# Squares on GpSimd, spread forms and a later S5 tile at the start of a hybrid decoder layer

## The chip, the cores and the metric

The kernel runs on one core of a Trainium2 chip. Its metric is the device time of one execution in microseconds (us), as the median of several executions. Five engines work side by side, each through its own instructions in order: TensorE (PE: matmuls, with PEld for its weight loads), VectorE (DVE), ScalarE (ACT), GpSimd (POOL) and SyncE (SP, which only issues transfers). ScalarE and GpSimd issue transfers as well.

## The reference

One layer of a decoder on 1024 prompt tokens and 8 sample tokens (1032 columns here), all in float32:

```python
h = rmsnorm(x, g_pre)                       # x * rsqrt(mean(x^2) + 1e-6) * g_pre, D = 2048
proj = h @ w_in                             # 2048 x 10240
q, k, v, za, ub, zb, ga, gb = split(proj)   # 4 x 1024, 2 x 1024, 2 x 2048 columns
ya = (retention(q, k, v) * silu(za)) @ w_pa
yb = (s5(ub) * silu(zb)) @ w_pb
out = (sigmoid(ga) * ya + sigmoid(gb) * yb) @ w_out
y = x + rmsnorm(out, g_post)
```

The states of retention and S5 are outputs too.

## The kernel before, in words

Activations lie transposed: a row tile is 128 features by 1032 tokens, and k counts the 16 such tiles of D. Each float32 product is made of three matmuls on rounded halves: a value is split into `hi` (a ScalarE copy that rounds) and `lo` (VectorE, value minus `hi`), and `three` issues hi x hi, hi x lo and lo x hi. Weights come as quarters of 128 x 512 (four k) and are split in the same way by `wtile`, into three rotating buffers a, b, c. The copy of a quarter can run once the matmuls of the quarter three before it are done.

Most of the kernel (`product`, line 984) multiplies with a Strassen-like scheme of seven products, which needs seven *forms* of the operands (`FORMS`: u1, t2, v1, t3, t1, t4, v2): halves of row tiles and sums and differences of them. What the change touches lies ahead of it, in the first 175 us:

1. The start stage (lines 382 to 411). It loads the 16 row tiles of x in the order `FX_ORDER`, splits each with the gain `g_pre` (L396 on ScalarE, L397 on VectorE), squares it on ScalarE (`sq`, L402, two buffers) and adds the square to `ssq`. TensorE multiplies each k at once with the weights of ub tiles 0 and 1 (weight tile j = 0, then j = 1, nine matmuls each). The normalisation is applied afterwards, as a scaling of the results by `rstd`. Six buffers `fx` hold row tiles; the last six stay for the forms.
2. `first_rms`, a generator of background work, computes `rstd`: nine small matmuls that read `ssq` (L461), a power on GpSimd (L467), two diagonal tiles on VectorE, matmuls that broadcast them (L477, L483), copies into `rstd`.
3. The second pair of row tiles: `linear` for ub tiles 2 and 3, four weight quarters each. After every third of the columns, and again at the end of a quarter, `slot()` runs the next piece of background work, up to its next `yield`: four slots a quarter, 32 in all. First `first_rms` runs in these slots and then `build_forms(0, ...)`. For each of four pairs of row tiles (u, v) that scales them (L423), makes t1 to t4 in four buffers `fo` (`tt`, counted as line 85), and stores seven forms to `fm_d`: u1, v1 and v2 by GpSimd's queue (L433), the t forms by ScalarE's (L437). Two row tiles, k = 0 and 3, are loaded again (`reload_a`, L448). After the first and the second pair, `scale_ub` scales ub tile 0 and ub tile 1 and stores it to `ub_d` for the S5 branch (L368); ub tiles 2 and 3 are stored by L351.
4. The v loop (`ps2`, lines 1309 to 1324): two tiles of v in eight quarters, with a slot at the end of each. Its background work is `first_forms`: it loads forms of the first half of K into ten buffers `stg` (`stage`, L923), waits four slots, and then splits four forms in a slot (`unstage`, L274), into the places that the row tiles of x leave. Product n of the first step (seven products) reads the n-th group of four.
5. The first step of `product`, from 157 us on; `first_forms` ends in its slots.

`slot()` lets background work be placed on TensorE, VectorE, ScalarE and SyncE only after the last foreground instruction there:

```python
def slot():
    with ExitStack() as after:
        for ins in anchor.values():
            after.enter_context(tc.issue_after(ins))
        while bg:
            try:
                next(bg[0])
                return
            except StopIteration:
                bg.popleft()
```

There is no such order for GpSimd. A helper such as `add` has all its instructions under line 85.

Of the kernel before, what the change touches and what calls it, by code (L numbers as in the profile page):

```python
# [10 lines left out]
F32 = mybir.dt.float32  # L11
F32R = mybir.dt.float32r
I32 = mybir.dt.int32
AF = mybir.ActivationFunctionType
ALU = mybir.AluOpType
# [3 lines left out]
D = 2048  # L19
SEQ = 1024  # L20
NB = 8
TOK = SEQ + NB
KD = D // 128
H = 8
G = 64
EPS = 1e-6
# [53 lines left out]
def emit(ctx, tc, I, O):  # L80
    nc = tc.nc
    V, A, P, T = nc.vector, nc.scalar, nc.gpsimd, nc.tensor
# [7 lines left out]
    def add(out, a, b, eng=None):  # L90
        return tt(out, a, b, ALU.add, eng)
# [16 lines left out]
    def st_tile():  # L108
        return stage_of["pool"].tile([128, stage_of["w"]], F32, name="st")
# [34 lines left out]
    fm_d = dram("fm_d", [2, 7, 4, 128, HT])  # L144
# [27 lines left out]
# [10 lines that stand above are left out]
# [54 lines left out]
    def misc():  # L236
        return banks_of["pms"].tile([128, 512], F32, name="misc")
# [90 lines left out]
    ubp = {}  # L328
# [5 lines left out]
        return t.rearrange("p (c s) -> p c s", s=8)  # L334

    def ub_new(j):
        u = ubp[j] = ubw.tile([128, 8, 144], F32, name="ubp")
        P.memset(u[:, 1:8, 0:8], 0.0)
        P.memset(u[:, 0:7, 136:144], 0.0)
        return u  # L340
# [22 lines left out]
    def scale_ub(j):  # L363
        u = ubp[j]
        mul(perm(u, 0, 128), perm(u, 0, 128), cs(rstd[:, 0:SEQ]))
        mul(u[:, 0, 0:8], u[:, 0, 0:8], rstd[:, SEQ:TOK])
        mul(u[:, 7, 136:144], u[:, 7, 136:144], rstd[:, SEQ:TOK])
        P.dma_start(ub_d[j * 128:(j + 1) * 128], u)  # L368
# [3 lines left out]

    s5stack = ExitStack()
    ubstack = ExitStack()
    ubw = ubstack.enter_context(tc.tile_pool(name="ubw", bufs=3))
    rm = ubstack.enter_context(tc.tile_pool(name="rm", bufs=1))
    ssq = rm.tile([128, TOK], F32, name="ssq")
    fx = ubstack.enter_context(tc.tile_pool(name="fxa", bufs=6))
    FX_ORDER = list(range(8, KD)) + [0, 3, 1, 2, 4, 5, 6, 7]
    kept = {}  # L380

    with tc.tile_pool(name="start", bufs=3) as sp:
        banks = [[mmbank() for _ in range(3)], [mmbank(), mmbank(), misc()]]
        w = None
        sqs = deque()
        for z, k in enumerate(FX_ORDER):
            xr = kept[k] = fx.tile([128, TOK], F32, name="fx")
            xh, xl = x_of(k)
            parts = THIRDS[0:3] if z == 0 else [(0, TOK)]
            for n, (a, b) in enumerate(parts):  # L390
                nc.sync.dma_start(xr[:, a:b], I["xT"][k, :, a:b])
                if z % 4 == 0 and n == 0:
                    w = [wquarter(w_in, M_UB, k // 4)]
                if z % 4 == 0 and n == len(parts) - 1:
                    w.append(wquarter(w_in, M_UB + 1, k // 4))
                A.activation(xh[:, a:b], xr[:, a:b], AF.Copy, scale=gpre[:, k:k + 1])  # L396
                V.scalar_tensor_tensor(xl[:, a:b], xr[:, a:b], gpre[:, k:k + 1], xh[:, a:b].bitcast(F32), ALU.mult, ALU.subtract)  # L397
            if z == 0:
                A.activation(ssq, xr, AF.Square)
            else:  # L400
                sqs.append(sp.tile([128, TOK], F32, name="sq", bufs=2))
                A.activation(sqs[-1], xr, AF.Square)  # L402
            for j in range(2):
                for t, (t0, t1) in enumerate(THIRDS[0:3]):
                    three(banks[j][t][:, 0:t1 - t0], w[j], k % 4, x_of(k), t0, t1, z == 0, z == KD - 1)
            if z > 1:
                add(ssq, ssq, sqs.popleft())
        add(ssq, ssq, sqs.popleft())
        for j in range(2):
            for t, (t0, t1) in enumerate(THIRDS[0:3]):  # L410
                evac_ub_raw(j, t, banks[j][t][:, 0:t1 - t0])
# [3 lines left out]
    def build_forms(kh, order, load, pool, fos, eng, after=()):  # L415
        raw = dict(kept) if not kh else {}
        load(raw, 0)
        yield
        for z, j in enumerate(order):
            t = {}  # L420
            for n, k in (("u", 8 * kh + j), ("v", 8 * kh + 4 + j)):
                r = raw.pop(k)
                V.scalar_tensor_tensor(r, r, gpre[:, k:k + 1], rstd, ALU.mult, ALU.mult)  # L423
                t[n + "1"], t[n + "2"] = r[:, 0:HT], r[:, HT:TOK]
            yield
            for n, a, b, op in (("t1", "u1", "u2", ALU.subtract), ("t3", "u2", "v2", ALU.subtract),
                                ("t2", "v2", "t1", ALU.add), ("t4", "v1", "t2", ALU.subtract)):
                t[n] = pool.tile([128, HT], F32, name="fo", bufs=fos)
                tt(t[n], t[a], t[b], op)
                if n == "t3":  # L430
                    for p, f in enumerate(FORMS):
                        if f in ("u1", "v1", "v2"):
                            eng.dma_start(fm_d[kh, p, j], t[f])  # L433
                    yield
            for p, n in enumerate(FORMS):
                if n[0] == "t":
                    A.dma_start(fm_d[kh, p, j], t[n])  # L437
            yield
            load(raw, z + 1)
            if z < len(after):  # L440
                after[z]()
            yield
# [10 lines left out]
                raw[k] = fb2.tile([128, TOK], F32, name="fx", bufs=4)  # L453
                P.dma_start(raw[k], I["xT"][k])

    def first_rms():
        n_ch = [(c, min(c + 128, TOK)) for c in range(0, TOK, 128)]
        r = TOK % 128
        ps = misc()
        for i, (a, b) in enumerate(n_ch):  # L460
            T.matmul(ps[0:b - a, i:i + 1], ssq[:, a:b], onesk, start=True, stop=True)  # L461
        ms, rs, hf = (rm.tile([128, 9], F32, name=n) for n in ("ms", "rs", "hf"))
        V.memset(ms, 1.0)
        V.memset(hf, -0.5)
        V.tensor_scalar(ms[:, 0:8], ps[:, 0:8], EPS, None, ALU.add)
        V.tensor_scalar(ms[0:r, 8:9], ps[0:r, 8:9], EPS, None, ALU.add)
        P.tensor_tensor(rs, ms, hf, ALU.pow)  # L467
        yield
        dg = [st_tile()[:, 0:512] for _ in range(2)]
        for i, d in enumerate(dg):  # L470
            V.scalar_tensor_tensor(d.rearrange("p (j c) -> p j c", c=128), ident.unsqueeze(1).broadcast_to([128, 4, 128]), float(D),
                                   rs[:, 4 * i:4 * i + 4].unsqueeze(2).broadcast_to([128, 4, 128]), ALU.mult, ALU.mult)
        yield
        yield
        for i, d in enumerate(dg):
            pb = misc()
            T.matmul(pb, onesk.broadcast_to([128, 128]), d, start=True, stop=True)  # L477
            V.tensor_copy(rstd[:, 512 * i:512 * i + 512], pb)
        d = st_tile()[0:r, 0:r]
        V.tensor_scalar(d, ident[0:r, 0:r], rs[0:r, 8:9], float(D), ALU.mult, ALU.mult)  # L480
        yield
        pb = misc()
        T.matmul(pb[:, 0:r], onesk[0:r, :].broadcast_to([r, 128]), d, start=True, stop=True)  # L483
        V.tensor_copy(rstd[:, SEQ:TOK], pb[:, 0:r])
        yield

    fb = ubstack.enter_context(tc.tile_pool(name="fb", bufs=1))
    bg.append(first_rms())
    bg.append(build_forms(0, (1, 2, 0, 3), reload_a, fb, 4, P, (lambda: scale_ub(0), lambda: scale_ub(1))))
    todo.extend((w_in, m, kq) for m in (M_UB + 2, M_UB + 3) for kq in range(4))  # L490
    todo.append((w_in, 16, 0))
    for j in (2, 3):
# [369 lines left out]
    def popen(name, side, bufs):  # L862
        st = ExitStack()
        return st, st.enter_context(tc.tile_pool(name=name, bufs=bufs, side=side))

    wstack, wst = popen("wst", "right", 7)
    estack, ev = popen("ev", "right", 2)
    gstack, stg = popen("stg", "left", 10)
    pairs = [("ub", 36), ("ub", 38)] + [("v", 18 + 2 * i) for i in range(3)] + [("za", 24 + 2 * i) for i in range(4)]
    for i in range(4):  # L870
        pairs += [("k", 8 + 2 * i), ("q", 2 * i)]
# [422 lines left out]
    order_q = [(n, i) for n in range(7) for i in range(4)]  # L1294

    def first_forms():
        for n, i in order_q[0:10]:
            stage(stg, "A", n, i)
        for _ in range(4):
            yield  # L1300
        for z, (n, i) in enumerate(order_q):
            unstage("A", n, i)
            if z + 10 < 28:
                stage(stg, "A", *order_q[z + 10])
            if z % 4 == 3:
                yield

    bg.append(first_forms())
    ps2 = [[mmbank() for _ in range(3)], [mmbank(), mmbank(), misc()]]
    with tc.issue_after(anchor["s"]):  # L1310
# [117 lines left out]
    for s in range(N2):  # L1428
        kh, p = steps[s]
        if s == 1:  # L1430
            drain()
            gstack.close()
            fstack, fb2 = popen("fb2", "left", 1)
            bg.append(build_forms(1, range(4), load_b, fb2, 4, A))
        if s == B0 - 2:
# [525 lines left out]
```

## Time and profile before

| | us |
|---|---|
| median of 3 runs | 2532.03 (2531.32 to 2534.67) |
| the profiled execution's own time | 2531.82 |
| its span, first to last instruction | 2530.0 |
| TensorE busy | 2499.5 |
| VectorE busy | 2010.4 |
| ScalarE busy | 998.1 |
| GpSimd busy | 770.0 |

The span is what the trace covers; the execution's own time has a little more around it. "Granted clock" is the share of TensorE's full clock that the chip let it have. A row of a time order gives start, duration, engine, line, operation, tiles (out<-in), shapes and, in brackets, how long the engine was idle before and what ended that.

### The profile page before, as it was taken

The numbers are of one execution on the slowest core, as the hardware profiler recorded it, in microseconds if no ns is written. First come the engines' busy times: TensorE is split into PE (matmuls) and PEld (weight loads), VectorE is DVE, ScalarE is ACT, GpSimd is POOL, SyncE is SP. The second block draws the span as 40 slices with busy tenths as digits, with TensorE's granted clock in tenths as the row PEclk, the third lists the DMA queues.
The fourth block names the chain that finished last, engine by engine and source line by source line (L and its number), as shares of the span: only waits on it lengthen the run. The fifth ranks groups of instructions, "written<-read, shape, count | busy, mean of one in ns | idle before, by whom it ended". The sixth has DMA issues, their size and how long they took to land.

```text
span 2530.0 us, 52856 instructions
## 1 busy us (share of the span) xinstructions
PE 2499.5 (99%) x20026; PEld 2451.7 (97%) x20026; DVE 2010.4 (79%) x4212; ACT 998.1 (39%) x1787; POOL 770.0 (30%) x1283
## 2 busy tenths in 40 slices
PE   9999999999999999999999999999999999999998
PEld 8999999999999999999999999999999999999976
DVE  7577789898898898768986767667897878989774
ACT  7042532333333333453334444445552422445532
POOL 0221323322222222223335444434332222433320
PEclk9999999999999999999999999999999999999999
DMA  5869865434444433788889888888888789856884
GB/s 194 269 203 307 237 168 159 129 126 132 127 130 137 129 125 125 223 212 220 216 218 261 229 227 229 211 226 238 277 288 280 228 238 319 299 191 163 220 293 136
DMA packets 243903, 527.59 MB, mean 209 GB/s; under 512 B 42832, under 2 KB 69664, under 8 KB 242880
## 3 DMA queue, kind: packets, MB, share of 16 engines
q0 software_dynamic: 104896, 306.53, 42.5%
q1 hardware_dynamic: 101536, 166.14, 20.9%
q10 hardware_dynamic: 37216, 51.54, 6.4%
q8 instruction: 158, 2.59, 0.4%
q14 instruction: 97, 0.79, 0.1%
HBM read 348.71 MB, written 175.37 MB: 207 GB/s over the span
## 4 chain that ended last, share of the span: by engine, by line
PE 74%; issue 4%; DVE 3%; DMA 2%; POOL 2%; ACT 0%; ACTq 0%; POOLq 0%; DVEq 0%; SPq 0%
PE acc L984 66%; PE acc L1859 3%; DMA wr<-in_w_outB 1%; PE misc L816 1%; PE misc L815 1%; PE misc L1209 1%; PE misc L1219 1%; PE misc L1188 1%; DMA a<-in_xT 1%; PE misc L766 1%; POOL zr L1678 1%; DMA a<-mg_d 1%; PE misc L1221 0%; DVE a L85 0%; DVE u L85 0%
## 5 line engine op out<-in xcount | busy, mean ns | idle before, releaser
L984 PE MATMUL acc<-a,whib 128*128 128x256 f32 (+1 forms) x3816 | 629.4, 284 | 4.0 <-DVE u L85 2.3
L984 PE MATMUL acc<-a,whic 128*128 128x256 f32 (+1 forms) x3808 | 628.6, 284 | 2.0 <-DVE u L85 1.4
L984 PE MATMUL acc<-a,whia 128*128 128x256 f32 (+1 forms) x3800 | 627.1, 284 | 0.5 <-ACT whia L965 0.5
L984 PEld LDWEIGHTS acc<-a,whib 128*128 128x128 f32 x3816 | 525.7, 188 | 6.6 <-ACT whia L965 4.3
L984 PEld LDWEIGHTS acc<-a,whic 128*128 128x128 f32 x3808 | 524.8, 188 | 7.3 <-issue 2.8
L984 PEld LDWEIGHTS acc<-a,whia 128*128 128x128 f32 x3800 | 524.0, 188 | 2.5 <-issue 1.0
L984 PE MATMUL acc<-a,wlob 128*128 128x256 f32 (+1 forms) x1908 | 396.9, 283 | 0.0
L984 PE MATMUL acc<-a,wloc 128*128 128x256 f32 (+1 forms) x1904 | 396.2, 283 | 0.4 <-DVE wloc L85 0.4
L984 PE MATMUL acc<-a,wloa 128*128 128x256 f32 (+1 forms) x1900 | 395.1, 282 | 0.0
L984 PEld LDWEIGHTS acc<-a,wloc 128*128 128x128 f32 x1904 | 297.7, 188 | 1.2 <-DVE wloc L85 1.2
L984 PEld LDWEIGHTS acc<-a,wlob 128*128 128x128 f32 x1908 | 298.3, 188 | 0.3
L984 PEld LDWEIGHTS acc<-a,wloa 128*128 128x128 f32 x1900 | 297.1, 188 | 0.0
L965 ACT CAST whic<-wraw 128x512 fp32r<-128x512 f32 x148 | 92.0, 621 | 232.2 <-PE acc L984 161.0
L965 ACT CAST whib<-wraw 128x512 fp32r<-128x512 f32 x146 | 90.7, 622 | 229.7 <-PE acc L984 172.6
L965 ACT CAST whia<-wraw 128x512 fp32r<-128x512 f32 x146 | 90.7, 621 | 220.1 <-PE acc L984 161.5
L85 DVE TENSOR_TENSOR wraw<-wr 128x512 f32<-128x512 f32 x220 | 150.8, 685 | 2.6
L85 DVE TENSOR_TENSOR wloc<-wraw,whic 128x512 fp32r<-128x512 f32 x156 | 106.8, 684 | 50.0 <-ACT whic L965 37.0
L965 ACT CAST whib<-wr 128x512 fp32r<-128x512 f32 x111 | 68.9, 621 | 194.3 <-PE acc L984 159.5
L85 DVE TENSOR_TENSOR wloa<-wraw,whia 128x512 fp32r<-128x512 f32 x154 | 105.4, 684 | 50.5 <-ACT whia L965 33.6
L85 DVE TENSOR_TENSOR a<-stg,a 128x516 fp32r<-128x516 f32 (+1 forms) x224 | 135.7, 637 | 10.6 <-ACT a L274 10.4
L965 ACT CAST whia<-wr 128x512 fp32r<-128x512 f32 x110 | 68.3, 621 | 190.9 <-PE acc L984 161.3
L965 ACT CAST whic<-wr 128x512 fp32r<-128x512 f32 x109 | 67.7, 621 | 186.0 <-PE acc L984 163.1
(472 smaller groups left out, 4236.5 us busy)
## 6 DMA issues: line engine op xcount, KB each, us to landing
wr<-in_w_in SPq DMA_DIRECT2D x296, 256.0 KB
pt_d<-u POOLq DMA_DIRECT2D x74, 258.0 KB, 3.1
u<-pt_d POOLq DMA_DIRECT2D x74, 258.0 KB, 5.2
wr<-in_w_out SPq DMA_DIRECT2D x64, 256.0 KB
wr<-in_w_outB SPq DMA_DIRECT2D x64, 256.0 KB
stg<-fm_d POOLq DMA_DIRECT2D x60, 258.0 KB, 4.1
pt_d<-st POOLq DMA_DIRECT2D x37, 258.0 KB, 3.6
pt_d<-p POOLq DMA_DIRECT2D x37, 258.0 KB, 3.0
```

The costliest lines, as they stand in the source:

```text
L85: return (eng or V).tensor_tensor(out, a, b, op)
L766: T.matmul(ps[:, q * 144:(q + 1) * 144], W1[:, g, :], U[:, g, :], start=True, stop=True)
L815: T.matmul(o, Tm[:, g, :], U[:, g, 0:136], start=True, stop=False)
L816: T.matmul(o, W3[:, g, 1:9, :], X[:, g, 0:136], start=False, stop=True)
L965: anchor["a"] = A.copy(hi, f).ins
L984: anchor["p"] = T.matmul(o, a[:, i, :], x, start=first and i == 0 and a is wh and b is xh, stop=n in (2, 5, 6) and i == 3 and a is wl, ski ...
L1188: T.matmul(ps[:, c * 128:(c + 1) * 128], kt[:, 4 * i + c, :], vt[:, 4 * i + c, :], start=True, stop=True)
L1209: T.matmul(ps[:, c * 128:(c + 1) * 128], kT[:, cs], qT[:, cs], start=True, stop=True)
L1219: T.matmul(o, S[:, n], vt[:, n], start=True, stop=n == 0)
L1678: P.dma_start(t, pt_d[2 * p + r, c, :, 0:HO], accum_op=ALU.add)
L1859: anchor["p"] = T.matmul(ps[c], a, b, start=k == 0 and a is xh and b is wh, stop=k == KD - 1 and a is xl).ins
```

## The change

- The square of each k after the first is added to `ssq` by GpSimd, at once; before, VectorE added it one k later.
- `first_rms` is defined earlier and queued inside the start stage: at the last k, between weight tile 0 and weight tile 1, a slot runs its first piece (the nine matmuls up to the power). Its other pieces are divided differently, and the small diagonal tile gets a buffer of its own.
- `build_forms` for the first half of K takes six slots for each pair of row tiles instead of four, and its t forms are stored by GpSimd's queue. The second half (`kh` = 1) is as before.
- ub tile 1 lies in a pool of its own, `ubk`, which stays open until step 1; its scaling and store become a piece of background work, `late_ub`, ahead of `first_forms`. The pool `ubw` has two buffers instead of three, and `stg` nine instead of ten.

```diff
-        u = ubp[j] = ubw.tile([128, 8, 144], F32, name="ubp")
+        u = ubp[j] = (ubk if j == 1 else ubw).tile([128, 8, 144], F32, name="ubp")
...
-    ubw = ubstack.enter_context(tc.tile_pool(name="ubw", bufs=3))
+    ubk_stack = ExitStack()
+    ubk = ubk_stack.enter_context(tc.tile_pool(name="ubk", bufs=1))
+    ubw = ubstack.enter_context(tc.tile_pool(name="ubw", bufs=2))
...
+    def first_rms():
+        ...                                     # nine matmuls of ssq, ms, hf
+        P.tensor_tensor(rs, ms, hf, ALU.pow)
+        yield
+        yield
+        dg = [st_tile()[:, 0:512] for _ in range(2)]
+        ...                                     # two diagonal tiles
+        de = rm.tile([r, r], F32, name="de")
+        V.tensor_scalar(de, ident[0:r, 0:r], rs[0:r, 8:9], float(D), ALU.mult, ALU.mult)
+        yield
+        for i, d in enumerate(dg):
+            pb = misc()
+            T.matmul(pb, onesk.broadcast_to([128, 128]), d, start=True, stop=True)
+            V.tensor_copy(rstd[:, 512 * i:512 * i + 512], pb)
+            if i == 0:
+                yield
+        ...                                     # the last eight columns
+        yield
...
-                sqs.append(sp.tile([128, TOK], F32, name="sq", bufs=2))
-                A.activation(sqs[-1], xr, AF.Square)
+                sq = sp.tile([128, TOK], F32, name="sq", bufs=2)
+                A.activation(sq, xr, AF.Square)
+                add(ssq, ssq, sq, P)
             for j in range(2):
+                if z == KD - 1 and j:
+                    bg.append(first_rms())
+                    slot()
...
-            if z > 1:
-                add(ssq, ssq, sqs.popleft())
-        add(ssq, ssq, sqs.popleft())
...
-            yield
+                if n == "v" or not kh:
+                    yield
...
                     yield
+                    if not kh:
+                        yield
...
-                    A.dma_start(fm_d[kh, p, j], t[n])
+                    (A if kh else P).dma_start(fm_d[kh, p, j], t[n])
...
-    bg.append(first_rms())
-    bg.append(build_forms(0, (1, 2, 0, 3), reload_a, fb, 4, P, (lambda: scale_ub(0), lambda: scale_ub(1))))
+    bg.append(build_forms(0, (1, 2, 0, 3), reload_a, fb, 4, P, (lambda: scale_ub(0),)))
...
-    gstack, stg = popen("stg", "left", 10)
+    gstack, stg = popen("stg", "left", 9)
...
+    def late_ub():
+        scale_ub(1)
+        yield
+
+    bg.append(late_ub())
     bg.append(first_forms())
...
             gstack.close()
+            ubk_stack.close()
```

In `first_forms` the two tens become nines.

More of the change, by code (lines that the diff above doesn't have):

```diff
@@ L380, in emit @@
     kept = {}
+    def first_rms():
+        n_ch = [(c, min(c + 128, TOK)) for c in range(0, TOK, 128)]
+        r = TOK % 128
+        ps = misc()
+        for i, (a, b) in enumerate(n_ch):
+            T.matmul(ps[0:b - a, i:i + 1], ssq[:, a:b], onesk, start=True, stop=True)
+        ms, rs, hf = (rm.tile([128, 9], F32, name=n) for n in ("ms", "rs", "hf"))
+        V.memset(ms, 1.0)
+        V.memset(hf, -0.5)
+        V.tensor_scalar(ms[:, 0:8], ps[:, 0:8], EPS, None, ALU.add)
+        V.tensor_scalar(ms[0:r, 8:9], ps[0:r, 8:9], EPS, None, ALU.add)
+        P.tensor_tensor(rs, ms, hf, ALU.pow)
[3 more added lines that the diff above has]
+        for i, d in enumerate(dg):
+            V.scalar_tensor_tensor(d.rearrange("p (j c) -> p j c", c=128), ident.unsqueeze(1).broadcast_to([128, 4, 128]), float(D),
+                                   rs[:, 4 * i:4 * i + 4].unsqueeze(2).broadcast_to([128, 4, 128]), ALU.mult, ALU.mult)
+        de = rm.tile([r, r], F32, name="de")
+        V.tensor_scalar(de, ident[0:r, 0:r], rs[0:r, 8:9], float(D), ALU.mult, ALU.mult)
+        yield
+        for i, d in enumerate(dg):
+            pb = misc()
[3 more added lines that the diff above has]
+                yield
+        pb = misc()
+        T.matmul(pb[:, 0:r], onesk[0:r, :].broadcast_to([r, 128]), de, start=True, stop=True)
+        V.tensor_copy(rstd[:, SEQ:TOK], pb[:, 0:r])
+        yield
     with tc.tile_pool(name="start", bufs=3) as sp:
@@ L384, in emit @@
         w = None
-        sqs = deque()
         for z, k in enumerate(FX_ORDER):
@@ L454, in load_b @@
                 P.dma_start(raw[k], I["xT"][k])
[L456 to L485, printed above, removed]
     fb = ubstack.enter_context(tc.tile_pool(name="fb", bufs=1))
-    bg.append(first_rms())
-    bg.append(build_forms(0, (1, 2, 0, 3), reload_a, fb, 4, P, (lambda: scale_ub(0), lambda: scale_ub(1))))
+    bg.append(build_forms(0, (1, 2, 0, 3), reload_a, fb, 4, P, (lambda: scale_ub(0),)))
     todo.extend((w_in, m, kq) for m in (M_UB + 2, M_UB + 3) for kq in range(4))
@@ L1296, in first_forms @@
     def first_forms():
-        for n, i in order_q[0:10]:
+        for n, i in order_q[0:9]:
             stage(stg, "A", n, i)
@@ L1302, in first_forms @@
             unstage("A", n, i)
-            if z + 10 < 28:
-                stage(stg, "A", *order_q[z + 10])
+            if z + 9 < 28:
+                stage(stg, "A", *order_q[z + 9])
             if z % 4 == 3:
                 yield
+    def late_ub():
+        scale_ub(1)
+        yield
+    bg.append(late_ub())
     bg.append(first_forms())
```

## The prediction

> **What bounds the kernel now.** I read the page's first part, then TensorE's waits, then the stretches around the one place where it waits long, and there the engines' own time order.
>
> ```profile
> PE 2499.5 (99%) x20026; PEld 2451.7 (97%) x20026; DVE 2010.4 (79%) x4212; ACT 998.1 (39%) x1787; POOL 770.0 (30%) x1283
> ```
>
> TensorE is busy for 2499.5 of 2530.0 us: 30.5 us are all that can be won without taking matmuls away, plus what matmuls lose at a lowered clock. So only a change that moves a wait of TensorE can move the time. Its waits after the start (line waited for: us in total, times, longest):
>
> ```profile
> PE mm L229 <- DVE wloa L85: 3.0, 1, 3.0
> PE mm L229 <- DVE wloc L85: 1.8, 1, 1.8
> PE acc L984 <- ACT whia L965: 0.6, 1, 0.6
> ```
>
> The first two lie in the second pair of row tiles (the `linear` loop over ub tiles 2 and 3). I cut that loop at the first matmul of each weight quarter and added three longer stretches:
>
> ```profile
> 80.52:86.15 5.63, 5.63 (x39) 5.63 (x37) 4.53 (x10) 0.62 (x1) 2.69 (x5) 1.00 1.00 311
> 86.15:95.45 9.30, 7.48 (x38) 7.16 (x37) 5.67 (x7) 0.62 (x1) 0.81 (x2) 0.82 1.04 351
> 95.45:105.88 10.43, 7.44 (x39) 7.12 (x38) 3.93 (x7) 0.62 (x1) 0.80 (x2) 0.84 0.84 270
> 105.88:111.51 5.63, 5.63 (x39) 5.63 (x37) 2.36 (x3) 0.62 (x1) 0.00 (x0) 1.00 0.74 199
> 68.00:102.00 34.00, 29.19 (x167) 28.54 (x166) 24.50 (x37) 2.93 (x5) 9.28 (x19) 0.90 0.97 313
> 111.00:157.00 46.00, 45.74 (x294) 45.53 (x292) 20.69 (x37) 13.66 (x25) 14.65 (x27) 1.00 0.70 233
> 157.00:175.00 18.00, 17.64 (x149) 17.68 (x150) 15.96 (x27) 11.07 (x21) 4.33 (x8) 1.00 0.48 158
> ```
>
> The columns are the stretch, its length, busy time of PE, PEld, DVE, ACT and POOL, the granted clock, the DMA share and GB/s. A quarter takes 5.63 us when nothing is late. Two took 9.30 and 10.43: 3.67 + 4.80 = 8.47 us too much. Waiting is 1.8 + 3.0 = 4.8 us of it; the other 3.7 us is the granted clock, 0.82 and 0.84 in those stretches, about 1.8 us for each stall. DMA is at its ceiling there (313 GB/s, share 0.97 over 34 us). What VectorE (first three rows) and ScalarE (last two) do then:
>
> ```profile
> 87.13 0.70 DVE L85 TENSOR_TENSOR fo<-fx 128x516 f32<-128x516 f32 x1 [2.08 <-DMA fm_d<-fo]
> 87.75 0.68 DVE L85 TENSOR_TENSOR wloc<-wraw,whic 128x512 fp32r<-128x512 f32 x1
> ...
> 97.61 0.70 DVE L85 TENSOR_TENSOR fo<-fx 128x516 f32<-128x516 f32 x1 [2.12 <-DMA fm_d<-fo]
> 98.23 0.68 DVE L85 TENSOR_TENSOR wloa<-wraw,whia 128x512 fp32r<-128x512 f32 x1
> ...
> 85.08 8.96 ACTq L437 DMA_DIRECT2D fm_d<-fo  x4
> 94.16 0.62 ACT L220 CAST whib<-wraw 128x512 fp32r<-128x512 f32 x1 [12.89 <-DMA fm_d<-fo]
> ```
>
> VectorE waits until a store of a form has left its `fo` buffer (four of them), and the low half of the weights, for which TensorE waits, stands behind that in its order. ScalarE's weight copies stand behind the same stores, which it issues: `whib` waited 12.9 us. So the stall is a bunching: four row tiles of forms in 16 slots of four quarters (22.5 us at 5.63 each), while their stores hold DMA at its ceiling for 34 us.
>
> **The change part by part.**
>
> *Forms spread, stores to GpSimd.* Each row tile takes 6 slots for 4, so 24 slots, six quarters, 33.8 us. The bytes stay the same. Work that ran 34 - 22.5 = 11.5 us behind its schedule now runs about 0.2 us behind. The lag that is gone is larger than the 8.47 us it cost, so I take all of it: -8.47. The other end of this term is 0, if the waits on `fo` only move. ScalarE loses 16 issues and the waits in front of them; GpSimd gains them:
>
> ```profile
> L437 ACTq DMA_DIRECT2D fm_d<-fo x16: 326/326/487, 69.3 to 101.1; - x16
> L433 POOL DMA_DIRECT2D fm_d<-fx x12: 539/542/728, 67.7 to 95.7; - x12
> ```
>
> 16 x 0.54 = 8.7 us more on GpSimd's queue, which had 9.28 us of work in 34: 0, hidden by its idle time. Behind those stores stand the two reloads of x, the ub stores and the memsets of the last ub tile; those memsets can hold the queue (3.5 us, row L338 below) and now hold form stores too. Only `fo`, hence VectorE, waits for that, and it has two quarters (11.3 us) before TensorE notices.
>
> *GpSimd adds the squares.* 15 additions leave VectorE, whose rows of the first stage are these (the last three from the time order of DVE, ACT and PE):
>
> ```profile
> L397 DVE SCALAR_TENSOR_TENSOR a<-fx,g_pre,a 128x1032 fp32r<-128x1032 f32 (+2 forms) x18 | 20.9, 1167 | 5.4 <-ACT a L396 5.4
> L396 ACT ACTIVATE a<-fx,g_pre 128x1032 fp32r<-128x1032 f32 (+2 forms) x18 | 18.7, 1054 | 2.7 <-DMA fx<-in_xT 1.9 <-DMA g_pre<-in_g_pre 0.8
> L85 DVE TENSOR_TENSOR ssq<-ssq,sq 128x1032 f32<-128x1032 f32 x15 | 18.4, 1225 | 0.0
> ...
> 10.67 1.29 DVE L397 SCALAR_TENSOR_TENSOR a<-fx,g_pre,a 128x1032 fp32r<-128x1032 f32 x1 [1.96 <-ACT a L396]
> ...
> 46.19 1.07 ACT L402 ACTIVATE sq<-fx 128x1032 f32<-128x1032 f32 x1 [1.94 <-DVE ssq L85]
> ...
> 52.32 0.33 PE L227 MATMUL mm<-a,whic 128*128 128x384 f32 x1
> ```
>
> VectorE is relieved of 18.4 us where TensorE does not wait for it, so nothing is won. But the sum now has a due time inside TensorE's stream: the nine matmuls that read `ssq` come ahead of the last k's second weight tile, at 52.32 us. The additions can start at about 11.9 us, behind the first split at 10.67; 15 of them fit if one takes at most (52.32 - 11.9) / 15 = 2.69 us, waits included. GpSimd has no such addition in this trace. Its nearest rows are memsets:
>
> ```profile
> L338 POOL MEMSET ubp<- 128x56 f32 x4 | 0.6, 141 | 3.8 <-DMA ub_d<-ubp 3.5 <-POOLq L1952 0.3
> ...
> L1447 POOL MEMSET z<- 128x112 f32 x1 | 0.2, 192 | 3.3 <-DVE a L85 3.3
> ```
>
> 56 more elements cost 51 ns, 0.91 ns each, over 90 ns. With all three streams of an addition side by side that is 1.03 us, with the two reads in turn 1.97, with all three in turn 2.91. I take 1.97, since a result can be written while the next operands are read: below 2.69, so the sum is ready by about 49.3 us (last square at 46.19 + 1.07, then one addition), 3.0 us early: 0. At 2.91 it would be 3.3 us late.
>
> The nine matmuls themselves, the power on GpSimd and the two broadcasts stay as many and only come earlier: 0.
>
> *One S5 tile later.* Scaling and storing ub tile 1 leaves the crowded stretch (2.0 us of VectorE, 0.54 of GpSimd, one 576 KB store) for the first slot of the v loop, where VectorE has 20.69 us of work in 46: 0 there. But it takes a slot ahead of the first forms, whose loads (nine buffers instead of ten) and splits come one slot later. One group of four splits slips into the first seven products:
>
> ```profile
> L85 DVE TENSOR_TENSOR a<-stg,a 128x516 fp32r<-128x516 f32 (+1 forms) x224 | 135.7, 637 | 10.6 <-ACT a L274 10.4
> ```
>
> 4 x 0.64 = 2.5 us more in 157 to 175, where VectorE has 15.96 of 18.00: 18.5, so 0.5 us too much. I take +0.5; the ends are 0 (evacuations wait instead of splits) and 2.5.
>
> **Sum.** -8.47 + 0 + 0.5 = -8.0. The profiled execution took 2531.82 us around its span of 2530.0, 0.2 under the median of 2532.03. So 2523.8 on its scale, 2524.0 on the median's.
>
> **The rivals.** *The additions and VectorE take turns* (slower side). There is a sign that GpSimd's reads wait for VectorE:
>
> ```profile
> 523.02 0.69 DVE L85 TENSOR_TENSOR wlob<-wr,whib 128x512 fp32r<-128x512 f32 x1
> 523.05 0.71 POOL L791 COPY fin<-X 128x4 f32<-128x4 f32 x1 [0.85 <-DVE X L85]
> ...
> 561.84 0.69 DVE L85 TENSOR_TENSOR u<-acc,p 128x516 f32<-128x516 f32 x1
> 561.88 0.19 POOL L791 COPY fin<-X 128x4 f32<-128x4 f32 x1 [3.13 <-DVE X L85]
> ```
>
> The same small copy takes 0.19 us beside a VectorE instruction with one input in PSUM, and 0.71, to that instruction's end, beside one with both inputs in SBUF. The splits L397 and the low halves of the weights have both inputs in SBUF. If they and the additions exclude each other for their whole length, the stage needs 15 x 1.167 + 6 x 0.68 = 21.6 us of VectorE and 15 x 1.97 = 29.6 us of GpSimd in turn, from 10.67 to 61.9: TensorE waits 9.5 us at `ssq` or before it, plus 1.8 for the clock. Net -8.0 + 11.3 = +3.3: 2535.3; at 2.91 us an addition 2549. It decides once addition and wait together exceed 2.69 us. Against it: no row shows VectorE waiting for GpSimd, and the copy does not tell how long a long read would hold.
>
> The Trainium skill, "SBUF — State Buffer", Who interferes with whom, states this rule: a VectorE instruction with two SBUF inputs and a GpSimd instruction that reads SBUF lock each other out, and the later one waits for the whole of the other. By that rule the copy at 523.05 should wait, and the trace agrees (0.71 against 0.19 us); its other direction no row here shows. The Trainium skill, "GPSIMD Engine Reference", Performance versus the Vector engine, measured 4497 ns for an addition of 2048 fp32 elements; scaled to 1032 that is an estimate of 2.27 us, by which alone the additions would still be in time, and in turn with VectorE the kernel would come out at 2539.8.
>
> *Part of a stall stays.* The forms still hold DMA near its ceiling, and the sum may be a little late: half of VectorE's share in every addition's wait (0.7 us) on 2.4 us, the middle of 1.97 and 2.91, gives 3.1 an addition and a sum 6.1 us late. One of the two stalls kept (3.67) gives 2527.7, the late sum 2530 to 2532. For it: the same bytes in 33.8 us are still 0.97 of the ceiling. Against: 11.3 us of slack.
>
> *The stall only moves.* If the bytes, not the slots, are what VectorE waits for, the wait moves to the v loop, where nine 258 KB loads and two 576 KB stores come together: 2532. Against: DMA share 0.70 from 111 to 157.
>
> **How the numbers follow.** Forecast (2522 to 2526): 0.47. Taking turns: 0.28, spread over 2534 to 2541. Part stays (2526 to 2532): 0.18. Only moves: 0.07. The range goes from 2522, where the 0.6 us wait goes too, to 2537, which takes in some four tenths of the taking-turns case and all of the middle ones: 0.83. About 0.2% (5.1 us) is what a measurement of this kernel can tell from no change: faster is below 2527.0, slower above 2537.1. Faster: 0.47 + 0.08 = 0.55. Slower: 0.17, of taking turns. Same: 0.28.
>
> **What would show it.** Right: no wait of TensorE between 60 and 105 us; quarters of 5.63 us and a granted clock of 1.00 there; GpSimd's additions at 2.0 to 2.6 us; `ssq` read at 52.3 without idle time; no `fm_d` issue from ScalarE before 160 us. Wrong: idle time of TensorE at the `ssq` matmuls, or splits L397 longer than 1.29 us or starting late in the first 50 us (turns); `fo` rows still ended by `fm_d` with TensorE waiting (part stays); a wait between 130 and 175 us on `a` or a weight above 2.5 us (the later slot).

## The result, and the profile after

The changed kernel takes 2549.15 us (median; 2545.98 to 2549.98) against 2531.68 us (2529.07 to 2534.67) of the kernel before: ratio 1.0067, 95% interval 1.0052 to 1.0083. It is slower by 17.5 us, where 8 us less were forecast. The profiled execution took 2549.98 us, its span is 2548.2 us, 18.2 more than before. First the busy times of the page, then the longest of TensorE's waits (line waited for: us in total, times, longest):

```profile
PE 2504.0 (98%) x20026; PEld 2454.1 (96%) x20026; DVE 2024.8 (79%) x4197; ACT 997.8 (39%) x1787; POOL 823.9 (32%) x1314
...
PE acc L989 <- DVE u L85: 5.8, 6, 2.9
PE mm L229 <- DVE wloa L85: 5.0, 1, 5.0
PE mm L227 <- ACT whib L220: 4.9, 1, 4.9
PE mm L228 <- DVE a L430: 4.5, 4, 3.1
PE mm L229 <- DVE wlob L85: 2.9, 1, 2.9
PE mm L229 <- DVE hf L392: 2.9, 1, 2.9
```

The 4.9 us at `whib` are the start of the program and stand there before and after (5.0). The waits for `wloa`, `a`, `wlob` and the one put down to `hf` are new, and all four lie in the start stage; the two of the second pair of row tiles are gone. (`hf` is a small memset of 0.07 us that ended 0.04 us after the low half `wloc`; the matmul reads `wloc`.) Cut by stage, with the columns of the stretches shown earlier, the kernel after reads:

```profile
10.00:53.00 43.00, 29.74 (x151) 27.81 (x152) 41.40 (x16) 31.90 (x34) 37.60 (x13) 0.88 0.54 195
53.00:78.39 25.39, 22.52 (x139) 22.15 (x138) 13.74 (x14) 5.77 (x10) 8.39 (x4) 0.93 0.09 32
78.39:171.53 93.14, 92.53 (x584) 91.08 (x583) 53.44 (x86) 18.06 (x33) 31.29 (x58) 1.00 0.75 246
```

and the kernel before, in the corresponding stretches of its start stage and from there to the first product:

```profile
10.00:53.72 43.72, 43.49 (x275) 42.88 (x274) 39.64 (x39) 35.94 (x41) 0.00 (x0) 1.00 0.58 211
53.72:157.35 103.63, 98.20 (x602) 96.10 (x601) 57.47 (x97) 20.93 (x38) 26.04 (x47) 0.97 0.72 234
```

From 10 us on TensorE was busy for 43.49 of 43.72 us before; it is busy for 29.74 of 43.00 us now, at a granted clock of 0.88, while VectorE is busy for 41.40 of them with 16 instructions instead of 39 (a wait inside an instruction counts as busy). It does less work in more time, and it has become the bound of that stage. The second pair begins at 78.39 us instead of 53.72, 24.67 later. About 2.0 of these are the work that moved there with the sum's matmuls (the same start comes at 55.75 us where VectorE keeps the additions, first experiment below), so 22.7 us are lost. From there to the first product it takes 93.14 us for 103.63: 10.49 less, the same 2.0 and the 8.47 of the two stalls. The rest of the program took 2376.7 us for 2372.7, 4.0 more. 22.7 + 2.0 - 10.5 + 4.0 = 18.2.

The groups of the first 80 us, with the columns of the groups shown earlier, name the loss:

```profile
L85 POOL TENSOR_TENSOR ssq<-ssq,sq 128x1032 f32<-128x1032 f32 x15 | 44.9, 2992 | 17.3 <-ACT sq L435 16.4
L430 DVE SCALAR_TENSOR_TENSOR a<-fx,g_pre,a 128x1032 fp32r<-128x1032 f32 (+2 forms) x18 | 41.0, 2315 | 6.3 <-ACT a L429 6.3
L435 ACT ACTIVATE sq<-fx 128x1032 f32<-128x1032 f32 x15 | 15.9, 1060 | 5.2 <-POOL ssq L85 5.2
```

The splits (now L430) take 41.0 us for 20.9, 2315 ns for 1167 each, with nothing changed in them. (ScalarE now waits 5.2 us in all for GpSimd to give the `sq` buffers free. TensorE does not pay for that: from 12.9 us to the low half `wloc` VectorE never stands idle, so nothing from ScalarE comes too late for it.) The time order of VectorE and of GpSimd shows them one by one:

```profile
45.47 3.23 POOL L85 TENSOR_TENSOR ssq<-ssq,sq 128x1032 f32<-128x1032 f32 x1
48.78 2.74 POOL L85 TENSOR_TENSOR ssq<-ssq,sq 128x1032 f32<-128x1032 f32 x1
...
46.40 2.85 DVE L85 TENSOR_TENSOR wloa<-wraw,whia 128x512 fp32r<-128x512 f32 x1
49.17 3.44 DVE L430 SCALAR_TENSOR_TENSOR a<-fx,g_pre,a 128x1032 fp32r<-128x1032 f32 x1
...
60.80 2.65 POOL L85 TENSOR_TENSOR ssq<-ssq,sq 128x1032 f32<-128x1032 f32 x1 [3.09 <-ACT sq L435]
61.14 3.41 DVE L430 SCALAR_TENSOR_TENSOR a<-fx,g_pre,a 128x1032 fp32r<-128x1032 f32 x1
64.47 0.68 DVE L85 TENSOR_TENSOR wloc<-wraw,whic 128x512 fp32r<-128x512 f32 x1
```

A low half of a weight quarter takes 2.85 us beside an addition and 0.68 once the additions are over: 2.2 us of waiting. A split takes 3.44 us beside one, 1.29 alone: 2.15. The additions wait too. Each of the 15 begins while a split or a low half is running, and counted from the end of that one, each takes 2.22 to 2.28 us: the addition at 48.78 ends at 51.52, 2.27 behind the end of `wloa` at 49.25. With its wait an addition takes 2.56 to 3.30 us, 3.23 in the median. Within each addition one VectorE instruction begins and stands until the addition is over, so the two go in turn. That cost VectorE some 31 us (20.1 in the splits, 11 in five low halves), and only 18.4 us of additions left it.

What TensorE pays is seen at one of its waits, and in the clock behind it:

```profile
49.31 0.69 PE L229 MATMUL mm<-a,wloa 128*128 128x384 f32 x1 [4.95 <-DVE wloa L85]
...
25.20:28.60 3.40, 3.14 (x10) 2.63 (x10) 3.40 (x2) 2.16 (x3) 3.32 (x2) 0.50 0.50 181
49.10:52.50 3.40, 3.19 (x11) 3.19 (x12) 3.40 (x2) 2.69 (x3) 3.32 (x2) 0.50 0.21 77
```

It idles for 16.15 us in eight places, of which four are long (3.06, 2.90, 4.95 and 2.87 us, ending at 25.1, 31.2, 49.3 and 65.2). Behind each of the four stands a stretch of some 3.4 us at half clock, two of them shown; together about 6.8 us lost. 16.15 + 6.8 = 22.95, against the 22.7 by the stage's end. (The first of the eight, 0.92 us at 10.9, waits for a row tile of x and not for an addition; the run with the forms spread alone has it too, 1.04 us at 11.0.)

### The profile page after: what moved, and what is told of

Same layout as the page of the kernel before. It is cut to its first block, busy times and chain, and to the rows that moved or that the text cites. A ratio compares the mean times of both kernels' runs of the same rounds, so it can differ in the third digit from the quotient of the medians.

```text
span 2548.2 us, 52845 instructions
## 1 busy us (share of the span) xinstructions
PE 2504.0 (98%) x20026; PEld 2454.1 (96%) x20026; DVE 2024.8 (79%) x4197; ACT 997.8 (39%) x1787; POOL 823.9 (32%) x1314
## 4 chain that ended last, share of the span: by engine, by line
PE 81%; issue 7%; DVE 5%; DMA 4%; POOL 3%; ACT 1%; POOLq 0%; DVEq 0%; ACTq 0%
PE acc L989 68%; PE acc L1870 3%; PE mm L229 2%; PE mm L227 1%; PE mm L228 1%; DMA u<-pt_d 1%; DMA wr<-in_w_outB 1%; DVE a L85 1%; DVE u L85 1%; PE misc L821 1%; PE misc L820 1%; PE misc L1224 1%; PE misc L1214 1%; PE misc L1193 1%; DMA a<-mg_d 1%
## 5 line engine op out<-in xcount | busy, mean ns | idle before, releaser
L85 DVE TENSOR_TENSOR wlob<-wraw,whib 128x512 fp32r<-128x512 f32 x154 | 109.9, 714 | 46.1 <-ACT whib L970 35.4
L85 DVE TENSOR_TENSOR a<-stg,a 128x516 fp32r<-128x516 f32 (+1 forms) x224 | 136.2, 640 | 10.9 <-ACT a L274 10.5
```

The costliest lines, as they stand in the source:

```text
L85: return (eng or V).tensor_tensor(out, a, b, op)
```

## The experiments

The theory: an addition on GpSimd and a VectorE instruction with both inputs in SBUF shut each other out, and this alone makes the loss; the forms and the later S5 tile are worth the 8.47 us. The rivals: the moved matmuls of the sum are what delays TensorE; the loss is in the forms' new order or in GpSimd's queue; any work of GpSimd at that time, not its reading, slows VectorE. That the VectorE instruction must have both inputs in SBUF is not tested below: all that ran beside the additions have. For it stands the prediction's row alone, the small copy that took 0.19 us beside an instruction with one input in PSUM.

**VectorE adds, the rest of the change stays**

```diff
-                sq = sp.tile([128, TOK], F32, name="sq", bufs=2)
-                A.activation(sq, xr, AF.Square)
-                add(ssq, ssq, sq, P)
+                sqs.append(sp.tile([128, TOK], F32, name="sq", bufs=2))
+                A.activation(sqs[-1], xr, AF.Square)
...
                 if z == KD - 1 and j:
+                    while sqs:
+                        add(ssq, ssq, sqs.popleft())
                     bg.append(first_rms())
                     slot()
...
+            if 1 < z < KD - 1:
+                add(ssq, ssq, sqs.popleft())
```

> The changed kernel with the additions of the squares back on VectorE (the last two ahead of the slot that reads the sum). Theory (GpSimd's additions and VectorE's two-input instructions take turns for their whole length): the first stage ends again at 53.7 us plus 1.9 us of sum matmuls, the stalls of the second pair stay gone, so 2531.7 - 8.5 = 2523.2 (2521 to 2526). Rival (the new place of the sum matmuls in TensorE's order is what costs): the first stage still ends near 78 us and the time stays above 2540.

Measured: 2527.84 us (2525.74 to 2530.5) against 2534.15 of the kernel before, ratio 0.9976 (0.9965 to 0.9986). Its groups of the first 80 us and its stretch of the start stage:

```profile
L431 DVE SCALAR_TENSOR_TENSOR a<-fx,g_pre,a 128x1032 fp32r<-128x1032 f32 (+2 forms) x18 | 21.0, 1174 | 5.5 <-ACT a L430 5.5
...
10.00:53.00 43.00, 43.00 (x273) 42.69 (x272) 39.65 (x39) 35.25 (x40) 0.00 (x0) 1.00 0.60 216
```

The splits are back at 1174 ns, TensorE is busy for all of the 43 us, and the second pair begins at 55.75 us. The early sum does no harm to the first stage. GpSimd's additions turned a gain into the loss: 2549.15 against 2527.84 us. The time is 1.8 us above the range that was expected; in the profiled execution the part behind the first product took 5.6 us longer than in the kernel before (see the rest of the program, below).

**GpSimd adds, nothing else is changed**

```diff
-                add(ssq, ssq, sqs.popleft())
+                add(ssq, ssq, sqs.popleft(), P)
```

(in both calls)

> The kernel before, with the 15 additions on GpSimd and nothing else. Theory (taking turns): the first stage ends some 22.8 us later and the two stalls of the second pair stay, so 2531.7 + 22.8 = 2554.5 (2550 to 2558). Rival (it is the new place of the sum matmuls): at most 2540.

Measured: 2555.61 us (2554.27 to 2562.25), ratio 1.0092 (1.0078 to 1.0106). The second pair begins at 72.33 us, 18.6 later than before, and both stalls of the forms are in their place behind it:

```profile
PE mm L229 <- DVE wloa L85: 3.8, 1, 3.8
PE mm L229 <- DVE wloc L85: 2.6, 1, 2.6
```

(TensorE's waits from 95 to 130 us.) So the loss comes with the additions alone, and the stalls stay with the forms' old slots and queue. At the second pair the loss is 4.1 us less than the 22.7 of the changed kernel, and TensorE's idle time up to there is 4.0 less, 12.15 for 16.15 us: three of the four long waits are there (3.05, 2.85 and 5.04 us), the fourth is not, because the low halves `wloc` (61.83) and `wloa` (62.43) run ahead of the last addition, which begins at 61.44 and takes 3.94 us; and two of the short waits at the start are missing. The second pair then takes 1.6 us longer than before (first product at 177.52 for 157.35), with stalls of 6.3 us for 4.8.

**Forms spread, nothing else is changed**

```diff
-            yield
+                if n == "v" or not kh:
+                    yield
...
                     yield
+                    if not kh:
+                        yield
```

> The kernel before with the forms of the first half of K on 6 slots a pair instead of 4, the t forms still stored by ScalarE. Theory (the bunching is what stalls TensorE): both stalls gone, 2523.2 (2521 to 2526). Rival (ScalarE, blocked by the stores that it issues, is what stalls): about half of the gain or none, 2527 to 2532.

Measured: 2524.3 us (2523.64 to 2524.5), ratio 0.9963 (0.9950 to 0.9975). From the second pair's start to the first product it takes 95.17 us, 8.46 less than before. It beats both kernels. Its median is the lowest of all versions run, but the intervals of the next two experiments overlap with its own.

**The t forms stored by GpSimd's queue, nothing else is changed**

```diff
-                    A.dma_start(fm_d[kh, p, j], t[n])
+                    (A if kh else P).dma_start(fm_d[kh, p, j], t[n])
```

> The kernel before with the t forms of the first half of K stored by GpSimd's queue, the slots as they were. Theory (bunching): VectorE still waits for the same stores, the stalls stay, 2529 to 2533. Rival (ScalarE blocked): ScalarE's copies come in time and the stalls go, 2523 to 2526.

Measured: 2526.47 us (2524.62 to 2528.46), ratio 0.9969 (0.9959 to 0.9980). The theory expected the stalls to stay; the rival was right. This alone takes away both stalls too, with the forms as bunched as before. The same stretch of 34 us as in the prediction, with the forms spread (first) and with the stores moved (second):

```profile
68.00:102.00 34.00, 34.00 (x219) 34.00 (x218) 25.10 (x37) 3.12 (x5) 9.57 (x19) 1.00 1.00 319
```

```profile
68.00:102.00 34.00, 34.00 (x219) 34.00 (x218) 25.87 (x39) 3.73 (x6) 16.48 (x31) 1.00 0.96 307
```

The DMA share is 1.00 and 0.96, as high as before (0.97), and TensorE is busy all the time. VectorE's and ScalarE's waits from 62 to 112 us, spread first, then with the stores moved:

```profile
DVE fo L85 <- DMA fm_d<-fo: 7.2, 7, 2.4
...
ACT whib L220 <- DVE fo L85: 18.5, 2, 9.5
ACT whia L220 <- DMA fm_d<-fo: 11.0, 1, 11.0
```

```profile
DVE fo L85 <- DMA fm_d<-fo: 6.8, 6, 4.6
...
ACT whib L220 <- PE mm L228: 15.1, 3, 7.2
```

VectorE still waits for stores, 7.2 and 6.8 us in all. With the forms spread ScalarE's weight copies still stand behind stores (11.0 us at one), but in time; with the stores moved the copies wait for nothing but weights and TensorE, and VectorE's wait of 4.6 us (up to 98.50) is covered, because the copies came in time and the three low halves stand ahead of it in VectorE's order, the last at 93.19. The stall needs both, bunched slots and the stores in ScalarE's order: VectorE's wait on `fo` does not make it alone, and with ScalarE's blocking besides it makes none in the spread slots.

**Both of these**

> The kernel before with both: 6 slots a pair and the t forms on GpSimd's queue; the sum, its place and ub tile 1 as before. Theory (bunching is all): 2523.2 (2521 to 2526), as the version with everything but the additions. Rival (the later ub tile 1 is needed as well): 2526 to 2530.

Measured: 2526.05 us (2524.09 to 2528.41), ratio 0.9968 (0.9957 to 0.9980), 0.05 us above the range that the theory expected. Its first product starts at 148.92 us, against 149.19 and 149.38 of the two alone: the two remedies don't add up. The first experiment, which has the later S5 tile and the earlier `first_rms` besides, has it at 148.89.

**What in the addition holds VectorE?** Three kernels take the first experiment, in which VectorE adds, and let GpSimd do something more for each square, whose result is not used (it goes into the buffer of ub tile 0, which is made ahead of the stage for this): a memset of 128x1024 that reads nothing (started by a copy of one element), a copy of 128x1024, which reads one operand, and an addition of 128x1024, which reads two.

```diff
+                P.tensor_copy(dum[:, 0:1, 0:1], sv[:, 0:1, 0:1])   # memset
+                P.memset(dum, 0.0)
...
+                P.tensor_copy(dum, sv)                             # copy
...
+                add(dum, sv, sv, P)                                # addition
```

> The version with the additions on VectorE, and beside each square an extra GpSimd memset of 128x1024 (behind a copy of one element that ties it to the square), result unused. Turns by reading alone: a memset reads nothing, so VectorE's splits stay at 1.29 us and the first stage ends near 55.6 us. Turns of any two instructions: splits over 2 us and a stage that ends over 5 us later.

> The same with an extra GpSimd copy of 128x1024 beside each square instead (one operand read), result unused. Turns by reading: each two-input instruction of VectorE that meets one waits up to the whole copy, about half of an addition (1.0 to 1.3 us), and the stage ends 8 to 16 us later, since VectorE has no room there. Turns only for two-operand instructions of GpSimd: no change, splits at 1.29 us.

> The same with an extra GpSimd addition of 128x1024 (two operands read), result unused, while VectorE adds the squares as well. Turns by reading: 2.1 us lost to each meeting, 36 two-input instructions of VectorE against 15 additions, so the stage ends 25 to 35 us later than 55.6. Rival (the loss in the changed kernel comes from ScalarE waiting for the sq buffers): under 10 us.

Measured, a single execution each: 2526.28, 2541.66 and 2553.51 us, with the second pair beginning at 56.23, 66.04 and 79.28 us. Groups of the first 80 us, the memsets first:

```profile
L434 DVE SCALAR_TENSOR_TENSOR a<-fx,g_pre,a 128x1032 fp32r<-128x1032 f32 (+2 forms) x18 | 20.9, 1172 | 6.2 <-ACT a L433 6.1
L442 POOL MEMSET ubp<- 128x1024 f32 x15 | 14.4, 958 | 0.9
```

then the copies:

```profile
L434 DVE SCALAR_TENSOR_TENSOR a<-fx,g_pre,a 128x1032 fp32r<-128x1032 f32 (+2 forms) x18 | 24.7, 1381 | 5.6 <-ACT a L433 5.6
L85 DVE TENSOR_TENSOR ssq<-ssq,sq 128x1032 f32<-128x1032 f32 x15 | 24.0, 1603 | 0.1
L441 POOL COPY ubp<-sq 128x1024 f32<-128x1024 f32 x15 | 23.1, 1543 | 36.3 <-ACT sq L439 36.3
```

and the additions:

```profile
L85 POOL TENSOR_TENSOR ubp<-sq 128x1024 f32<-128x1024 f32 x15 | 38.2, 2546 | 33.6 <-ACT sq L439 33.3
L85 DVE TENSOR_TENSOR ssq<-ssq,sq 128x1032 f32<-128x1032 f32 x15 | 33.4, 2228 | 0.1
L434 DVE SCALAR_TENSOR_TENSOR a<-fx,g_pre,a 128x1032 fp32r<-128x1032 f32 (+2 forms) x18 | 27.3, 1528 | 4.2 <-ACT a L433 4.2
```

15 memsets of 958 ns leave the splits at 1172 ns, and VectorE's additions too keep their time. The copies lengthen VectorE's two groups by 3.7 and 5.5 us (against 21.0 and 18.5 in the first experiment), the additions by 6.3 and 14.9. So it is GpSimd's reading instructions that hold VectorE, not its being busy or its writing, and an addition holds it longer than a copy. That the start of the second pair moves by 0.5, 10.3 and 23.5 us follows the same order. (Expected were 8 to 16 us for the copies, at 1.0 to 1.3 us a meeting, and 25 to 35 for the additions, at 2.1; a copy holds 0.78 and this addition 1.70.)

## Why the prediction was wrong, point by point

**GpSimd adds the squares: 0.** This is the step that failed. It held the price of an addition, 1.97 us, against the threshold of 2.69 us "waits included", and counted no wait into the price. The addition's own time is 2.22 to 2.28 us, 0.3 above the 1.97 and below the threshold; with its wait it is 3.23 in the median, above it. And the step priced no wait of VectorE at all, where there were some 31 us. Its threshold looked at the wrong reader: it asked when the sum would be ready, but the sum was never waited for. `ssq` is complete at 63.45 us (60.80 + 2.65), 11.1 us behind the due time of 52.32, not 3.0 ahead; but TensorE itself came so late that its matmuls read it at 75.0:

```profile
L389 PE MATMUL misc<-onesk,ssq x18: 163/250/250, 75.0 to 76.8; 128*128 128x1 f32 x16, 128*8 128x1 f32 x2
```

What was late were the splits and the low halves of the weights, on VectorE, which TensorE reads at every k.

**The rival that additions and VectorE take turns** was right in mechanism, and its chance of 0.28 too low. The sign that it rested on, the small copy of 0.71 us for 0.19, held at full length in both directions. The rule of the Trainium skill, "SBUF — State Buffer", Who interferes with whom, in which the later one of two such instructions waits for the other, agrees with the splits of 3.44 us beside an addition and 1.29 alone; in the memsets' run, where GpSimd reads next to nothing, VectorE is not held, as that rule has it for instructions that read SBUF. The estimate of 2.27 us from the Trainium skill, "GPSIMD Engine Reference", Performance versus the Vector engine, agrees with the 2.22 to 2.28 us of an addition counted without its wait.

Its price was too low as well: +11.3 us in the stage at 1.97 us an addition, 22.7 measured. The end of the turn-taking was nearly right (61.9 us forecast; the last addition ends at 63.45). But the price let TensorE run undisturbed up to `ssq` and charged one wait and one drop of the clock, 9.5 + 1.8 us. In fact it waited in eight places, lost clock behind four of them, and at 65.2 us it still had its last matmuls up to 75.0 to do. At the addition's own 2.27 us the same working gives a wait of 14.0 us and, with 1.8 for the clock, 15.8: 2539.8 in all, as the prediction says. TensorE's idle time of 16.15 us is near that wait; what is missing is the clock, 6.8 us for 1.8. The price of 2549 us at 2.91 an addition meets the measured time by luck: the 2.91 is 0.6 too high, and 4.0 us of the measured time lie in the rest of the program, which it leaves out.

**Forms spread, stores to GpSimd: -8.47.** Right in size: 95.17 for 103.63 us with the spreading alone. In the changed kernel the quarters of the second pair take 5.63 or 5.64 us each from the third on. But the reason was only half of it: a bunching of slots makes no stall when ScalarE does not issue the stores, and the part's two halves do the same thing twice.

**One S5 tile later: +0.5.** No cost shows where the term had it, which is the term's lower end, 0: TensorE's only wait from 130 to 200 us is the 0.6 us at `whia` that was there before. No run changes the later tile alone, so what it does further on is not shown.

**The first_rms work that moves: 0.** Right; the 2.0 us by which the start stage grows are gone from the second pair.

**The rest of the program: not forecast.** 4.0 us of the 18.2 lie behind the first product. TensorE waits 5.8 us there for `u` (before 3.7; the waits that the prediction lists end at 250 us and leave these out). In their profiled executions the kernels differ from the one before in this part by 0.6 to 8.0 us, without any order that follows the change: 0.6 with the forms spread, 5.6 with VectorE's additions restored, 8.0 with the extra copies; and executions of one kernel differ by 1 to 8 us in all. What sets it was not tried and stays open. It does not decide the sign: the 14.2 us at the first product do.

**What would have shown it.** The prediction named the sign itself: splits longer than 1.29 us in the first 50 us. They are.

## What to carry to other kernels

Before work is moved to GpSimd to relieve VectorE, ask which instructions VectorE runs at that time: with two inputs in SBUF they and GpSimd's reads go in turn, so the time of GpSimd's instruction is added to VectorE's, here 2.2 us for an addition that took VectorE 1.23. Price a late operand at every place where it is read, not once at the end of the stage, and each longer wait of TensorE with the half clock behind it. Of two remedies for one stall try each alone: here each did all of it, and both together gained no more.

## What the runs showed of the hardware that was not expected

- GpSimd holds VectorE only with an instruction that reads SBUF, and then for nearly its whole time. A memset of 128x1024 (958 ns) cost nothing. A copy, 0.91 us without its wait, made a split take 2.06 us for 1.28 (+0.78); an addition of 128x1024, 1.75 us, made an addition of VectorE take 2.92 for 1.22 (+1.70). The changed kernel's own additions, of 1032 columns and in place, 2.27 us, cost +2.15 to +2.2. Why the two kinds of addition differ by 0.5 us was not tried.
- GpSimd waits as well: the copy of one element in the memsets' run took 1047 ns in the mean (0.19 at the least), and all 15 end 0.04 or 0.05 us behind the end of one of VectorE's splits, low halves or additions:

```profile
L441 POOL COPY ubp<-sq 128x1 f32<-128x1 f32 x15 | 15.7, 1047 | 17.8 <-ACT sq L439 17.6
```

- In the changed kernel four waits of TensorE of 2.9 to 5 us each brought one stretch of some 3.4 us at half clock, about 1.7 us of work lost each, the same as the 1.8 us behind the two stalls before. The four short waits of 0.24 to 0.93 us at the stage's start, at 10.9 to 19.0 us, brought none: the granted clock is 1.00 from 10.9 to 22 us. The length of a wait does not decide alone: the 1.82 us before 88.5 us in the kernel before brought half clock, 2.08 us before 44.9 us in the run with the extra additions did not (1.00 from 44.9 to 52 us). And a stretch can be longer: in the run where only the additions were moved, the clock is 0.50 from 23.8 to 34.0 us, over two waits.
